# A hybrid attention and RWKV-7 block: the last v projection, the last bonus' split tiles and the first loads of attention and scans change their places

## The chip, the cores and the metric

One core of a Trainium2 chip runs the whole block in one launch. The metric is the device time of one launch in microseconds (us). Lower is better. The profile of an execution also has a span, which is the time from its first to its last recorded instruction. Five engines work side by side: PE multiplies matrices, DVE and ACT work elementwise, POOL (GpSimd) does a few elementwise operations and issues some transfers, and SP issues most transfers. Each engine runs its own instructions strictly in their order; the order is fixed when the kernel is compiled.

## The reference, cut to what matters

```python
h = rms_norm(x, norm_mix)
proj = h @ w_in                      # columns: q, k, v | r, k, v, low ranks | gates
attn = windowed_gqa(q, k, v, sink)   # 8 query heads, 2 key heads, blocks of 128 tokens +-128
zr = zr + shift_mu * (centred_shift(zr) - zr)
rw = rwkv7_time_mix(zr, ...)         # forward and backward scan of 64-wide states, plus
#   bonus = einsum(r, k_dir, r_k) * v
gates = sigmoid(proj[..., O_GATE:])  # 2 x 1024 columns
merged = gates[0] * (attn @ w_up_attn) + gates[1] * (rw @ w_up_rwkv)
x = x + merged @ w_out
x = x + square(relu(rms_norm(x) @ w_ff1)) @ w_ff2
x = x + (p @ w_ple) * sigmoid(rms_norm(x) @ w_ple_gate)
```

There are 1,024 tokens of width 1,024, all in float32. A product is made from three products of split operands (high times high, high times low, low times high), so each weight tile is first split into two parts, `hi` by ACT and `lo` by DVE or POOL.

## The kernel before, in words

The kernel goes through its stages in this order: norm and q, k, v; RWKV preparation; attention; the scans; the merge; the two feed-forward products; the per-layer embedding. The change lies in the end of the preparation and the beginning of the attention, at about 240 to 490 us of the span.

**Preparation.** A loop `for p in range(NP)` treats four pairs of heads (p = 0 to 3). Per pair there are three projections of 48 matmuls each: keys k, receptances r and values v. `shifted` empties their PSUM banks through ACT into the tile `zr` (room for two) and DVE adds the shift. `low_rank` makes the decays and rates, `direction(0, p, ...)` and `direction(1, p, ...)` make each scan direction's operands on DVE and ACT and write them out as `ra_d` and `bk_d`, 1 MB each. `add_bonus` first splits `rk` through `sums2` into high and low halves, multiplies them by ones on PE, transposes v for `v_d`, and writes `bv_d`. The second half's split tiles `s2h` and `s2l` lie in the room `gth` of pool `PW`, which has two places.

**Weights.** `load_proj` loads a projection's weights into pool `PW`, which has two places for split weights and two for the raw halves. `weights_ahead` starts, behind one projection, the load of a later one by the table `ahead2`. For p below 3 that table has k, r and v. For p = 3 it has none of them, so the last v projection loads its weights when it comes up.

**Gate products.** `gates(0)` makes 16 blocks of 24 matmuls each from weights of its own through the same places of `PW`; each block's tanh `gth` lies in the room `gth` until its transfer to `g_d` is done. `fill0` draws matmuls from this generator at fixed places of the last pair, p = 3: before the change 56 ahead of `direction(0, 3)` and the v projection, 56 behind the second `low_rank`, and 12 at each of four loads of `kT`. That makes 160. The rest (and one block of the second half) has the lowest priority and is placed by the compiler between the attention's own work.

**Attention.** Its tiles open in the room of the preparation, after the last bonus' last transfer. It runs over 8 blocks `n`. Its first loads are the queries `qT` (issued by POOL), the mask `band` and the logits `sink` (issued by ACT before the change), and the values `V` (SP). `low_products` loads `la` and `lb` and multiplies them for the scans' first inverse; its loads and those of the scans' first operands (`rac`, `bkc`) are traced at block 3, and nothing binds them to a place in SP's queue. The put of a block's output is the transfer `at_d`.

The program's order is a priority; a compile-time planner makes each engine's fixed order out of it. `after(a, b)` places `a` behind `b` on one engine, and no engine waits for it at run time.

Of the kernel before, what the change touches and what calls it, by code (L numbers as in the profile page):

```python
# [9 lines left out]
F32 = mybir.dt.float32  # L10
F32R = mybir.dt.float32r
# [6 lines left out]
P = 128  # L18
# [6 lines left out]
NP = 4  # L25
NH = 8
# [5 lines left out]
EPS = 1e-6  # L32
LOW = 1000000
X1AT = 5
BQ = 'scalar'
WOAT = (0, 4)

NFS = {2: "s0", 3: "c0 s1", 4: "t0 c1 t1 s2 c2", 5: "t2 s3 c3", 6: "t3 s4 c4", 7: "s5 c5"}
# [11 lines left out]
N1AT = 5  # L50
SQPIN = (1, 2, 3, 4, 5, 6, 7)
TPB = 2
F0 = (56, 56, 12)

FILL0 = 4

# [81 lines left out]
def block_kernel(ctx: ExitStack, tc: tile.TileContext, I: dict, out: bass.AP):  # L138
    nc = tc.nc

    def pool(stack, name, bufs=1, **kw):
        return stack.enter_context(tc.tile_pool(name=name, bufs=bufs, reuse_waits="tile", **kw))
# [9 lines left out]
    ra_d = DR.tile([ND, NCH, P, NP, P], F32, name="ra_d")  # L152
    bk_d = DR.tile([ND, NCH, P, NP, P], F32, name="bk_d")
# [3 lines left out]
    at_d = DR.tile([P, NP, T], F32, name="at_d")  # L157
# [20 lines left out]
    def after(ins, prev):  # L178

        tc.add_manual_dep(  # L180
            ins.ins, prev.ins.name,
            mybir.DependencyInfo(mybir.DependencyClass.NoSync, mybir.DependencyReason.DATA),
            reason="keep_in_program_order")
# [4 lines left out]
    def split(hi, lo, src, lo_eng=None, pin=False):  # L188

        a = nc.scalar.copy(hi, src)  # L190
        b = (lo_eng or nc.vector).tensor_tensor(out=lo, in0=src, in1=hi.bitcast(F32), op=ALU.subtract)  # L191
        if lo_eng is nc.gpsimd:
            on_pool[0] = b
        if pin:
            tc.keep_in_program_order(a)
            tc.keep_in_program_order(b)
# [78 lines left out]
    ahead2, ready = {}, {}  # L275
    for p in range(NP):
        k_, r_, v_ = (O_RWKV + o_ + p * P for o_ in (512, 0, 1024))
        if p < NP - 1:
            ahead2[k_], ahead2[r_], ahead2[v_] = v_, k_ + P, r_ + P

    def load_proj(c):
        ready[c] = load_w(PW, "w", w_in[:, :, c:c + P], P, parts=2, lo_eng=nc.vector)
# [40 lines left out]
    with ExitStack() as s0:  # L323
# [45 lines left out]
        qkn = QW.tile([P, 648], F32, name="qkn")  # L369
# [52 lines left out]
        for t in range(NT):  # L422
# [3 lines left out]
            if t == NT - 1:  # L426
                sA.close()
                PW = pool(sW, "wA", side="right")
# [65 lines left out]
    one_r = G.tile([P, P], F32R, name="one_r")  # L494
# [7 lines left out]
    with ExitStack() as s1:  # L502
        A1 = pool(s1, "prep")
# [82 lines left out]

        s2 = A1.tile([P, 2, 512], F32R, name="s2")

        def sums2(w, src):

            halves = []
            for h in range(2):
                hs = slice(512 * h, 512 * h + 512)
                if h:
                    hi, lo = (PW.tile([P, 512], F32R, name=n, tag="gth", bufs=2) for n in ("s2h", "s2l"))
                else:
                    hi, lo = s2[:, 0], s2[:, 1]
                split(hi, lo, src[:, hs])
                halves.append((hs, hi, lo))
            yield  # L600
            pss = []
            for hs, hi, lo in halves:
                ps = PX.tile([P, 512], F32, name="px", tag="px", bufs=6)
                nc.tensor.matmul(ps, w, hi, start=True, stop=False)
                nc.tensor.matmul(ps, w, lo, start=False, stop=True)
                pss.append((hs, ps))
            yield pss

        def add_bonus(p, rk, vz):
            sums = sums2(one_r, rk)  # L610
            next(sums)
            yield

            vt = A1.tile([P, NT, P], F32, name="vt", bufs=1)
            for q in range(2):
                tp = PX.tile([P, 4, P], F32, name="vtp", tag="px", bufs=6)
                for j in range(4):
                    nc.tensor.transpose(tp[:, j, :], vz[:, (4 * q + j) * P:(4 * q + j + 1) * P], ident)
                nc.scalar.copy(vt[:, 4 * q:4 * q + 4, :], tp)
            nc.sync.dma_start(v_d[:, p * P:(p + 1) * P].rearrange("(t q) c -> q t c", q=P), vt)  # L620
            bv = A1.tile([P, T], F32, name="bv", tag="vt", bufs=1)
            for hs, ps in next(sums):
                nc.vector.tensor_tensor(out=bv[:, hs], in0=ps, in1=vz[:, hs], op=ALU.mult)
            nc.sync.dma_start(bv_d[p], bv)
            yield
# [3 lines left out]
        def fill0(p, i):  # L629

            if p == NP - 1:
                for _ in range(F0[i]):
                    next(gates0)
# [15 lines left out]
        def keys(p):  # L649

            kz = shifted(O_RWKV + 512 + p * P, 4 + p)
            nc.scalar.activation(out=nrm[:, 0], in_=kz, func=AF.Square, scale=col("k_k", p))
            sums = sums2(one_r, nrm[:, 0])
            next(sums)
            return kz, sums
# [65 lines left out]
        for p in range(NP):  # L721
            if bonus:
                next(bonus)

            fill0(p, 0)
            rk = A1.tile([P, T], F32, name="rk", bufs=1)
            direction(0, p, *ops, rk)
            vz = shifted(O_RWKV + 1024 + p * P, 8 + p, proj_with(O_RWKV + 1024 + p * P, {VH: lambda: bonus and next(bonus)}))
            th, ta = low_rank(p, 1)
            fill0(p, 1)  # L730
            nxt = keys(p + 1) if p + 1 < NP else None
            direction(1, p, decays(1, th), ta, *ops[2:], rk)
            bonus = add_bonus(p, rk, vz)
            if nxt:
                ops = normed_keys(p + 1, *nxt)

        kT = PY.tile([P, 2, 2, T], F32R, name="kT", tag="yk")
        for q in range(4):
            ts = slice(256 * q, 256 * q + 256)
            a = nc.gpsimd.dma_start(kT[:, :, :, ts], kT_d[:, :, :, ts])  # L740
            if q:
                after(a, on_pool[0])
            fill0(NP - 1, 2)
        for _ in bonus:
            pass

# [6 lines left out]
    def chunk(s, d):  # L753
        return s if d == 0 else NCH - 1 - s
# [5 lines left out]
        nc.gpsimd.memset(z[64:96, :, 32:64], 0.0)  # L760
        return z

    def low_products(pl, ps_of, b, mm):

        def load(ci):
            la, lb = ([pl.tile([P, NP, 64], F32, name=n, bufs=4) for _ in range(ND)] for n in ("la", "lb"))
            for d in range(ND):
                c = chunk(NB * b + ci, d)
                nc.sync.dma_start(la[d], ra_d[d, c][:, :, 0:64])
                nc.sync.dma_start(lb[d], bk_d[d, c][:, :, 64 * d:64 * d + 64])  # L770
            return la, lb

        nxt = load(0)
        yield
        lt = pl.tile([P, 32, 64], F32, name="lt", bufs=1)
        for ci in range(NB):
            la, lb = nxt
            pss = [ps_of([P, NP, 64], "lps") for _ in range(2)]
            for j in range(NP):
                for q in range(2):  # L780
                    for d in range(ND):
                        e = q ^ d
                        rows = slice(64 * e, 64 * e + 64)
                        l_, r_ = (lb, la) if d == 0 else (la, lb)
                        mm(pss[e][own[d], j, :], l_[d][rows, j, :], r_[d][rows, j, :], start=True, stop=True)
            for e in range(2):
                nc.scalar.copy(lt[:, 8 * ci + e:8 * ci + 8:2, :], pss[e])
            if ci + 1 < NB:
                nxt = load(ci + 1)
            yield lt  # L790
# [60 lines left out]
    BI = pool(sB, "inv")  # L851
    BP = pool(sB, "prod")

    NRA, NBK = 4, 3
    ra_t, bk_t = {}, {}
# [8 lines left out]
    operand_tiles(BP, (0, 1), (0,))  # L864

    def load_ra(s, d):
        nc.sync.dma_start(ra_t[s % NRA, d], ra_d[d, chunk(s, d)])

    def load_bk(s, d):
        nc.sync.dma_start(bk_t[s % NBK, d], bk_d[d, chunk(s, d)])  # L870

    lts, zzs, lows = {}, {}, {}
    with ExitStack() as s2:
        A2 = pool(s2, "att")
# [5 lines left out]
        def queries(n):  # L880
            qT = A2.tile([P, NH, P], F32R, name="qT", bufs=2)
            nc.gpsimd.dma_start(qT, qT_d[n])
            return qT

        qT0 = queries(0)
        low0 = low_products(BI, ps_att, 0, nc.tensor.matmul)
        band = A2.tile([P, 3, P], F32, name="band")
        getattr(nc, BQ).dma_start(band, I["band"])
        V = A2.tile([P, NT, P], F32, name="V")
        nc.sync.dma_start(V, va_d.rearrange("(t q) c -> q t c", q=P))  # L890
        A3 = A2
        sink = A3.tile([P, NH], F32, name="sink")
        getattr(nc, BQ).dma_start(sink, I["qkn"][:, 640:648].partition_broadcast(P))
        nsink = A3.tile([P, NH], F32, name="nsink")
        nc.vector.tensor_scalar_mul(nsink, sink, -1.0)
        for n in range(NT):
# [5 lines left out]
            for kv in range(2):  # L902
# [3 lines left out]
                sums = A3.tile([P, 4], F32, name="sums", bufs=2)  # L906
                es = A3.tile([P, 4], F32, name="es", bufs=2)
                sm = A3.tile([P, 4, 3 * P], F32, name="smk", bufs=2)
                for h in range(4):
                    sc = PA.tile([P, nk * P], F32, name="sc", tag="sc", bufs=2)  # L910
                    for j in range(2):
# [3 lines left out]
                        scalar=-3.0e38, op0=ALU.add, op1=ALU.max, accum_out=mx[:, h:h + 1])  # L915
# [25 lines left out]
                    nc.tensor.matmul(po[kv * 64:kv * 64 + 64], V[:, k0 + j, kv * 64:kv * 64 + 64], pTs[kv][:, j, :, :], start=(j == 0), stop=(j == nk - 1))  # L941
            at = A3.tile([P, 4, P], F32, name="at", bufs=1)
            nc.scalar.copy(at, po)
            nc.sync.dma_start(at_d[:, :, n * P:(n + 1) * P], at)
            if n == 1:
                zi = zi_tile(BI, "zi")
            if n == LOW_AT:
                lts[0] = list(low0)[-1]
                for d in range(ND):
                    load_ra(0, d)  # L950
                    load_bk(0, d)
            if n == INV_AT:
                zzs[0] = inverse_turned(BI, inverse(BI, lts[0]))
        with tc.high_priority(offset=-LOW):
# [293 lines left out]
    for s in range(NCH):  # L1248
# [39 lines left out]
        if s % NB == NB - 1 and s // NB < 3:  # L1288
            b = s // NB + 1
# [615 lines left out]
```

## Time and profile before

| | |
|---|---|
| Median of three runs | 1773.99 us (1770.4 to 1774.12) |
| The profiled execution: its time and its span | 1774.3 us, 1772.5 us |
| PE busy | 1683.0 us, 95% |
| DVE busy | 1139.9 us, 64% |
| ACT busy | 895.5 us, 51% |
| POOL busy | 212.8 us, 12% |
| Mean granted TensorE clock | 0.978 of full speed |

The execution's own time is 1.8 us longer than its span. PE's busy time counts matmuls whose ends are modelled, so 95% doesn't say that PE is at its peak, but it says that PE is seldom empty. The waits of PE are few, and they can be looked up one by one.

### The profile page before, as it was taken

The numbers are of one execution on the slowest core, as the hardware profiler recorded it, in microseconds if no ns is written. First come the engines' busy times: TensorE is split into PE (matmuls) and PEld (weight loads), VectorE is DVE, ScalarE is ACT, GpSimd is POOL, SyncE is SP. The second block draws the span as 40 slices with busy tenths as digits, with TensorE's granted clock in tenths as the row PEclk, the third lists the DMA queues.
The fourth block names the chain that finished last, engine by engine and source line by source line (L and its number), as shares of the span: only waits on it lengthen the run. The fifth ranks groups of instructions, "written<-read, shape, count | busy, mean of one in ns | idle before, by whom it ended". The sixth has DMA issues, their size and how long they took to land. (4 is left out here: it accounts for less than half of the span.)

```text
span 1772.5 us, 29961 instructions
## 1 busy us (share of the span) xinstructions
PE 1683.0 (95%) x11544; PEld 1353.8 (76%) x11544; DVE 1139.9 (64%) x1977; ACT 895.5 (51%) x1636; POOL 212.8 (12%) x210
## 2 busy tenths in 40 slices
PE   7999999799999989898889989999999999999998
PEld 7987776565587777776668867888888888888887
DVE  6658994376928383956662587776776877685432
ACT  5548885277655646474621454444444444554221
POOL 3330000411221221121322000000000000000000
PEclk9999999899999999988989989999999999999999
DMA  6354654855264454355653305444447973574111
GB/s 213 92 133 125 186 159 144 247 148 137 71 181 138 130 142 127 109 162 173 210 187 120 131 32 195 154 148 156 155 144 275 307 246 114 180 225 144 53 42 43
DMA packets 274239, 269.20 MB, mean 152 GB/s; under 512 B 47920, under 2 KB 196272, under 8 KB 274096
## 3 DMA queue, kind: packets, MB, share of 16 engines
q1 hardware_dynamic: 263872, 253.98, 46.1%
q0 software_dynamic: 9792, 12.59, 2.7%
q8 instruction: 91, 1.49, 0.4%
q10 hardware_dynamic: 432, 0.73, 0.1%
q14 instruction: 52, 0.43, 0.1%
HBM read 186.49 MB, written 80.74 MB: 151 GB/s over the span
## 5 line engine op out<-in xcount | busy, mean ns | idle before, releaser
L1787 PE MATMUL ff2ps<-tl,sh 128*128 128x512 f32 x448 | 174.4, 389 | 0.0
L1787 PE MATMUL ff2ps<-th,sl 128*128 128x512 f32 x448 | 174.3, 389 | 0.0
L1787 PE MATMUL ff2ps<-th,sh 128*128 128x512 f32 x448 | 173.9, 389 | 0.0
L191 POOL TENSOR_TENSOR wlo<-wst,whi 128x512 fp32r<-128x512 f32 x66 | 89.1, 1361 | 259.7 <-ACT whi L190 228.1
L190 ACT CAST sh<-sst 128x512 fp32r<-128x512 f32 x109 | 67.8, 622 | 102.4 <-PE ff2ps L1787 56.9
L175 POOL TENSOR_TENSOR rstd<-ms,neghalf 128x1 f32<-128x1 f32 x24 | 13.3, 555 | 792.3 <-DVE ms L173 792.3
L191 DVE TENSOR_TENSOR sl<-sst,sh 128x512 fp32r<-128x512 f32 x109 | 75.1, 689 | 46.9 <-ACT sh L190 46.6
L1787 PEld LDWEIGHTS ff2ps<-tl,sh 128*128 128x128 f32 x448 | 84.1, 188 | 18.0 <-DVE tl L191 0.4
L1787 PEld LDWEIGHTS ff2ps<-th,sh 128*128 128x128 f32 x448 | 84.0, 188 | 17.6 <-ACT th L190 0.3
L1787 PEld LDWEIGHTS ff2ps<-th,sl 128*128 128x128 f32 x448 | 84.1, 188 | 17.5
L190 ACT CAST whi<-wst 128x512 fp32r<-128x512 f32 x100 | 59.7, 617 | 55.6 <-DMA wst<-in_w_in_dram 23.0
L190 ACT CAST w1h<-w1st 128x512 fp32r<-128x512 f32 x48 | 28.4, 620 | 103.8 <-DMA w1st<-in_w_ff_dram 63.9
L191 DVE TENSOR_TENSOR w1l<-w1st,w1h 128x512 fp32r<-128x512 f32 x48 | 31.8, 688 | 50.7 <-ACT w1h L190 50.7
L1112 DVE TENSOR_TENSOR gm<-gps,gmask 128x512 f32<-128x512 f32 x64 | 42.2, 684 | 28.3 <-PE gps L213 28.3
L223 PE MATMUL gmm<-hh,wlo 128*128 128x512 f32 x136 | 56.2, 413 | 1.0 <-DVE wlo L191 0.7
L219 PE MATMUL gmm<-hh,whi 128*128 128x512 f32 x136 | 55.8, 410 | 1.3 <-ACT gth L316 1.3
L221 PE MATMUL gmm<-hl,whi 128*128 128x512 f32 x136 | 56.6, 416 | 0.0
L807 DVE TENSOR_TENSOR tmp<-Lp,Z 128x31 f32<-128x31 f32 (+15 forms) x124 | 52.0, 420 | 4.6 <-POOL Z L802 1.8
L191 DVE TENSOR_TENSOR w1l<-ssum,w1h 128x512 fp32r<-128x512 f32 x64 | 43.0, 687 | 16.1 <-ACT w1h L190 16.1
L1537 PE MATMUL ff1ps<-fh,w1l 128*128 128x512 f32 x128 | 51.0, 399 | 0.6 <-DVE w1l L191 0.6
L1537 PE MATMUL ff1ps<-rh,w1h 128*128 128x512 f32 x128 | 50.0, 391 | 1.7 <-ACT w1h L190 1.7
L213 PE MATMUL gmm<-hh,wlo 128*128 128x512 f32 x120 | 51.3, 428 | 0.0
(410 smaller groups left out, 4937.3 us busy)
## 6 DMA issues: line engine op xcount, KB each, us to landing
wst<-in_w_in_dram SPq DMA_DIRECT2D x92, 256.0 KB, 3.4
tst<-in_w_ff_dram SPq DMA_DIRECT2D x80, 256.0 KB, 4.0
w1st<-in_w_ff_dram SPq DMA_DIRECT2D x32, 512.0 KB, 5.1
hid_S<-h SPq DMA_DIRECT2D x64, 256.0 KB, 2.1
sst<-hid_S SPq DMA_DIRECT2D x64, 256.0 KB, 2.8
hid_A<-h SPq DMA_DIRECT2D x48, 256.0 KB, 2.1
sst<-hid_A SPq DMA_DIRECT2D x45, 256.0 KB, 3.8
ra_d<-ra SPq DMA_DIRECT2D x8, 1024.0 KB, 5.7
```

What stands on the lines that cost most here:

```text
L175: nc.gpsimd.tensor_tensor(out=r, in0=ms, in1=neghalf.broadcast_to([P, width]), op=ALU.pow)
L190: a = nc.scalar.copy(hi, src)
L191: b = (lo_eng or nc.vector).tensor_tensor(out=lo, in0=src, in1=hi.bitcast(F32), op=ALU.subtract)
L213: tc.keep_in_program_order(nc.tensor.matmul(*a, **kw))
L219: mm(ps, ah, bh, start=(i == 0), stop=False)
L221: mm(ps, ah, bl, start=False, stop=False)
L223: mm(ps, al, bh, start=False, stop=(i == n - 1))
L807: nc.vector.tensor_tensor(out=tv, in0=Lp[:, t + 1:32, t:t + 1].broadcast_to([P, n, m]), in1=Z[:, t:t + 1, 0:m].broadcast_to([P, n, m]), op ...
L1112: nc.vector.tensor_tensor(out=gm[d][:, s % NB, q::2, :], in0=pss[q], in1=gmask[:, d, :].unsqueeze(1).broadcast_to([P, NP, P]), op=ALU.mult)
L1537: nc.tensor.matmul(ps, x_[:, k, :], y_[:, k, :], start=start and k + i == 0, stop=k == 3 and i == 2, skip_group_check=True)
L1787: nc.tensor.matmul(banks[bs][i], x_[:, isl], y_, start=fresh and p + j == 0, stop=p == NPR - 1 and j == 2, skip_group_check=True)
```

## The change

Four edits belong to it. The last v projection's weights are loaded behind the last k projection (`ahead2` gets `k_` for p = 3 too). The first 56 of the gate products move from ahead of `direction(0, 3)` to behind the second `low_rank`, so that 112 stand there. The last bonus' `s2h` and `s2l` go from the room `gth` to the room `zr` of pool `A1`. `band` and `sink` are issued by SP ahead of everything else of the attention, the scans' `la` and `lb` loads stand behind the put of block 0, and the first `rac` and `bkc` loads behind that of block 3.

```diff
-F0 = (56, 56, 12)
+F0 = (112, 12)
...
     for p in range(NP):
         k_, r_, v_ = (O_RWKV + o_ + p * P for o_ in (512, 0, 1024))
+        ahead2[k_] = v_
         if p < NP - 1:
-            ahead2[k_], ahead2[r_], ahead2[v_] = v_, k_ + P, r_ + P
+            ahead2[r_], ahead2[v_] = k_ + P, r_ + P
...
-        def sums2(w, src):
+        def sums2(w, src, pool_tag=(PW, "gth")):
...
-                    hi, lo = (PW.tile([P, 512], F32R, name=n, tag="gth", bufs=2) for n in ("s2h", "s2l"))
+                    hi, lo = (pool_tag[0].tile([P, 512], F32R, name=n, tag=pool_tag[1], bufs=2) for n in ("s2h", "s2l"))
...
-            sums = sums2(one_r, rk)
+            sums = sums2(one_r, rk, (A1, "zr") if p == NP - 1 else (PW, "gth"))
...
-            fill0(p, 0)
             rk = A1.tile([P, T], F32, name="rk", bufs=1)
             direction(0, p, *ops, rk)
             vz = shifted(O_RWKV + 1024 + p * P, 8 + p, proj_with(O_RWKV + 1024 + p * P, {VH: lambda: bonus and next(bonus)}))
             th, ta = low_rank(p, 1)
-            fill0(p, 1)
+            fill0(p, 0)
...
-            fill0(NP - 1, 2)
+            fill0(NP - 1, 1)
...
-    def low_products(pl, ps_of, b, mm):
+    def low_products(pl, ps_of, b, mm, behind=None):
...
-                nc.sync.dma_start(la[d], ra_d[d, c][:, :, 0:64])
-                nc.sync.dma_start(lb[d], bk_d[d, c][:, :, 64 * d:64 * d + 64])
+                for a in (nc.sync.dma_start(la[d], ra_d[d, c][:, :, 0:64]),
+                          nc.sync.dma_start(lb[d], bk_d[d, c][:, :, 64 * d:64 * d + 64])):
+                    if behind:
+                        after(a, behind)
...
+        band = A2.tile([P, 3, P], F32, name="band")
+        nc.sync.dma_start(band, I["band"])
+        sink = A2.tile([P, NH], F32, name="sink")
+        nc.sync.dma_start(sink, I["qkn"][:, 640:648].partition_broadcast(P))
         qT0 = queries(0)
-        low0 = low_products(BI, ps_att, 0, nc.tensor.matmul)
-        band = A2.tile([P, 3, P], F32, name="band")
-        getattr(nc, BQ).dma_start(band, I["band"])
         V = A2.tile([P, NT, P], F32, name="V")
         nc.sync.dma_start(V, va_d.rearrange("(t q) c -> q t c", q=P))
...
-            nc.sync.dma_start(at_d[:, :, n * P:(n + 1) * P], at)
+            put = nc.sync.dma_start(at_d[:, :, n * P:(n + 1) * P], at)
+            if n == 0:
+                low0 = low_products(BI, ps_att, 0, nc.tensor.matmul, put)
+                next(low0)
...
                 for d in range(ND):
-                    load_ra(0, d)
-                    load_bk(0, d)
+                    for a in (load_ra(0, d), load_bk(0, d)):
+                        after(a, put)
```

## Rows read from the trace of the kernel before

**Rows 1.** The page's chain that ended last: shares of the span by engine.

```profile
PE 46%; DVE 1%; ACT 0%; DMA 0%; issue 0%; POOL 0%; DVEq 0%; ACTq 0%; POOLq 0%
```

**Rows 2.** Waits of PE, 250 to 500 us: total us, times, longest us.

```profile
PE px L604 <- ACT s2h L190: 8.3, 1, 8.3
...
PE mm L219 <- ACT whi L190: 2.3, 1, 2.3
PE gmm L219 <- ACT gth L316: 1.3, 1, 1.3
...
PE gmm L223 <- DVE wlo L191: 0.7, 1, 0.7
```

**Rows 3.** Windows: stretch, length, busy PE PEld DVE ACT POOL, PEclk, DMA, GB/s.

```profile
250.00:260.00 10.00, 10.00 (x45) 7.61 (x44) 10.00 (x9) 8.21 (x12) 0.00 (x0) 1.00 0.69 209
...
326.00:341.20 15.20, 6.87 (x19) 4.77 (x18) 1.98 (x3) 3.70 (x7) 2.50 (x2) 0.67 0.90 262
...
350.60:493.00 142.40, 130.60 (x718) 85.28 (x716) 101.62 (x322) 97.24 (x256) 30.62 (x32) 0.96 0.46 131
```

**Rows 4.** Timeline of ACT and of its own transfer queue (ACTq).

```profile
334.30 0.62 ACT L190 CAST s2h<-rk 128x512 fp32r<-128x512 f32 x1 [9.70 <-DMA g_d<-gth]
...
346.33 0.33 ACTq L888 DMA_DIRECT2D band<-in_band_dram  x1
```

**Rows 5.** Timeline of DVE.

```profile
322.22 1.23 DVE L715 TENSOR_TENSOR rk<-rk,z 128x1024 f32<-128x1024 f32 x1
...
339.35 1.29 DVE L623 TENSOR_TENSOR bv<-px,z 128x512 f32<-128x512 f32 x2 [3.57 <-DMA v_d<-vt]
...
353.11 0.17 DVE L895 TENSOR_SCALAR nsink<-sink 128x8 f32<-128x8 f32 x1 [12.47 <-DMA sink<-in_qkn_dram]
```

**Rows 6.** Windows of the gate matmuls alone: length, PE busy, PEclk, DMA, GB/s.

```profile
303.00:326.00 23.00, 21.38 (x89) 1.00 0.72 188
...
336.40:350.50 14.10, 14.07 (x51) 0.83 0.81 261
```

**Rows 7.** Timeline of PE: start us, us, what, [idle before <- releaser].

```profile
265.63 0.40 PE L219 MATMUL gmm<-hh,whi 128*128 128x512 f32 x1
...
290.30 0.80 PE L219 MATMUL mm<-hh,whi 128*128 128x512 f32 x1 [2.30 <-ACT whi L190]
...
293.45 0.42 PE L219 MATMUL mm<-hh,whi 128*128 128x512 f32 x1
...
301.98 1.09 PE L213 MATMUL px<-lr,wlrh 128*128 128x512 f32 x4
...
325.21 1.04 PE L618 MATMUL vtp<-ident,z 128*128 128x128 f32 x8
...
334.97 0.79 PE L604 MATMUL px<-s2h,one_r 128*128 128x512 f32 x1 [8.25 <-ACT s2h L190]
...
341.13 0.48 PE L219 MATMUL gmm<-hh,whi 128*128 128x512 f32 x1
...
350.56 0.63 PE L912 MATMUL sc<-kT,qT 128*128 128x256 f32 x4
...
353.78 0.51 PE L912 MATMUL sc<-kT,qT 128*128 128x256 f32 x2 [2.12 <-DVE mx L913]
```

**Rows 8.** Timeline of SP's transfer queue.

```profile
335.92 0.37 SPq L620 DMA_DIRECT2D v_d<-vt  x1
...
341.14 0.38 SPq L624 DMA_DIRECT2D bv_d<-bv  x1
```

**Rows 9.** Timeline of POOL.

```profile
344.24 1.12 POOL L882 DMA_DIRECT2D qT<-qT_d  x2
```

**Rows 10.** DMA issues, 326 to 352 us: count, KB each, median us to landing.

```profile
band<-in_band_dram ACTq DMA_DIRECT2D x1, 192.0 KB, 6.0
```

**Rows 11.** Instructions that read tile la: ns min/median/max, first to last start us.

```profile
L785 PE MATMUL lps<-la,lb x34: 218/218/267, 408.0 to 416.7; 64*64 64x64 f32 x34
```

**Rows 12.** Instructions of line 944, the puts of the attention's blocks.

```profile
L944 SPq DMA_DIRECT2D at_d<-at x8: 525/558/622, 369.0 to 485.5; - x8
```

More of the change, by code (lines that the diff above doesn't have):

```diff
@@ L34 @@
 X1AT = 5
-BQ = 'scalar'
 WOAT = (0, 4)
@@ L866, in load_ra @@
     def load_ra(s, d):
-        nc.sync.dma_start(ra_t[s % NRA, d], ra_d[d, chunk(s, d)])
+        return nc.sync.dma_start(ra_t[s % NRA, d], ra_d[d, chunk(s, d)])
     def load_bk(s, d):
-        nc.sync.dma_start(bk_t[s % NBK, d], bk_d[d, chunk(s, d)])
+        return nc.sync.dma_start(bk_t[s % NBK, d], bk_d[d, chunk(s, d)])
     lts, zzs, lows = {}, {}, {}
@@ L891, in block_kernel @@
         A3 = A2
-        sink = A3.tile([P, NH], F32, name="sink")
-        getattr(nc, BQ).dma_start(sink, I["qkn"][:, 640:648].partition_broadcast(P))
         nsink = A3.tile([P, NH], F32, name="nsink")
```

## The prediction

> **What bounds the kernel now.** The first view is the page's chain of work. Its shares add up to 47% and nearly all of it is PE [rows 1]. 47% of the span of 1772.5 us is some 833 us, so the chain ends, followed back, at about 940 us. It says that the second half of the kernel waits for PE alone. It says nothing of the preparation's end, which lies at 265 to 350 us. So the second view is the list of PE's waits there [rows 2]. Two of them are large, and both belong to things that the change touches: 8.3 us at the last bonus' second product, which waits for the high part `s2h`, and 2.3 us at the last v projection, which waits for its weights. The third view, the windows, shows what that does: from 326 to 341.2 us PE works for 6.87 of 15.2 us, at 0.67 of its clock, while DVE (1.98 us) and ACT (3.70 us) are nearly empty too [rows 3]. All engines stand still for one thing. The fourth view is ACT's timeline, which names it: the cast of `s2h` waits 9.70 us for the transfer `g_d<-gth`, since `s2h` needs a place in the room `gth` that a gate's tanh leaves only when it has been written out [rows 4]. `rk`, from which `s2h` is made, was ready at 322.22 + 1.23 = 323.45 us [rows 5]. It is the room that is late and not the data.
>
> **Is time won here won at the end?** From 350.6 to 493 us PE is busy for 130.6 of 142.4 us, DVE for 101.62 and ACT for 97.24 [rows 3]. PE's remaining 11.8 us are spread over many small waits. Whatever starts the attention earlier moves this stretch as a whole, because the same work follows: the number of gate matmuls drawn before it is 160 before and after the change (56 + 56 + 48, and 112 + 48). The scans and everything behind them follow in their fixed order. So I let a gain here pass to the end in full.
>
> **The change part by part.**
>
> *Price of a matmul and of the clock.* 89 gate matmuls took 21.38 us at full clock, 0.240 us each [rows 6]. Behind the 2.30 us gap PE starts 7 matmuls from 290.30 to 293.45 us, so 0.450 us each, 0.210 more: 7 x 0.210 = 1.47 us. That is the price of the 1.2 GHz level against 2.4 GHz there. Behind the 8.25 us gap 13 starts lie between 334.97 and 341.13 us [rows 7], 6.16 us where 13 x 0.240 = 3.12 would do, so 3.04 us.
>
> *The last v projection.* With `ahead2` for p = 3 its weights follow the k projection's, in the places that the first gate block's weights have now, and those were in time. So the 2.30 us and the 1.47 us behind them go: 3.77 us. The 56 moved matmuls cost the same at either place. The wait of 1.3 us for a tanh [rows 2] belongs to the same crowding: that tanh stands on ACT behind the previous bonus' copies, which will now fall into the v projection. I count 1.31 us as gone; the bounds are 0 and 1.31.
>
> *What moves forward with it.* The second `low_rank` now stands at 301.98 us, and `rk` is ready 21.5 us later, at 323.45 [rows 5, 7]. After the change it follows the v projection directly: r's product ends and the gates begin at 265.63 [rows 7], v takes 48 x 0.240 = 11.5, the bonus inside it 1.04 + 4 x 0.240 = 2.0, so `low_rank` begins at about 279 and `rk` is ready at about 301. The bonus itself keeps its place behind 160 gate matmuls. These begin behind `low_rank` (1.09 us for its first half, some 1.8 in all), and 160 x 0.240 = 38.4 us later it is 319. The bonus now begins at 325.21 [rows 7]. `rk` has some 18 us to spare.
>
> *The cost of that.* The lo parts of the first five gate blocks are made on DVE, and four of them now meet `direction(1, 3)` there. The nearest row is the wait for such a part, 0.7 us [rows 2]. Four such waits would cost 2.7 us, none 0; the splits are traced first and so have priority, and I take 1.0.
>
> *The bonus' room.* The room `zr` is free when the bonus comes: its two places were last used by the r and v projections, whose shift is over by about 282 us (279 and two operations of 1.23 us on DVE). So the 8.25 us and the 3.04 us behind them go: 11.29 us. The gates get both places of `gth` back, which I count at nothing, because no other wait for that room is in the list.
>
> *The attention's start.* It opens when `bv_d` has landed. From the issue of `v_d` at 335.92 over `bv` at 339.35, `bv_d` at 341.14 and `qT` at 344.24 to the first score at 350.56 it takes 14.64 us [rows 5, 7, 8, 9]. PE has 51 gate matmuls to cover it [rows 6], 12.2 us at full clock. Now they run partly at the lower clock and last 14.07. So a wait of up to 14.64 - 12.2 = 2.4 us can show in front of the first score, and with it up to 1.47 us of clock. With less of a queue of transfers (DMA share 0.90 now [rows 3]) all four landings may come earlier, and then it is 0. I take 1.5 of 0 to 3.9 us.
>
> *`band` and `sink`.* ACT issues them at 346.33 us, 2.09 us after POOL issues the queries at 344.24 [rows 4, 9], because a tanh stands ahead of them on ACT. DVE waits for them until 353.11 [rows 5], and PE's third score waits 2.12 us for DVE [rows 7]. Issued first by SP they go out with the queries, so I count 2.09 us and, as behind the 2.30 us gap, 1.47 us of clock. The bounds are 0 and 3.6.
> The transfer of `band` took 6.0 us on ACT's own queue [rows 10]. The Trainium skill, "DMA: Bandwidth & Descriptors", section "Queues, rings and completion order", says that every DMA engine takes turns between the queues, while within one queue descriptors are consumed in ring order. That speaks against the move: behind two weight loads of 256 KB in SP's queue `band` would, by an estimate from that page's rule and 262 GB/s [rows 3], land 2.0 us later, and the sum would be smaller by the 3.6 us of this item: 1760.5 instead of 1757. No row shows `band` on SP's queue.
>
> *The scans' loads.* `la` and `lb` are read from 408.0 us [rows 11]; behind the first put, at 369.0 [rows 12], they have 39 us. `rac` and `bkc` come behind block 3's put and are used by the scans, behind the last put at 485.5 [rows 12]. The cover is the attention itself. Without it a load would cost a landing like that of `band`, 6.0 us. On SP the weights of the next gate blocks move up, which I count at nothing.
>
> *Sum.* -3.77 - 1.31 + 1.0 - 11.29 + 1.5 - 2.09 - 1.47 = -17.4 us. From the profiled execution's 1774.3 us that makes 1756.9; I say 1757. The median of the runs, 1773.99, differs from that execution by 0.3 us.
>
> **The rivals.**
>
> *A. The wait changes its name.* PE's gap stays in part: the first score or the gate blocks' weights wait where `s2h` did. For it: after the bonus SP's queue holds loads that need the attention's room, and weights behind them wait as well. `bv_d` goes out 5.2 us behind `v_d`, and the room opens 3.1 us later [rows 8, 9]: 8.3 us. Against it: the weights in front of `V` now pass in time. Of the 17.4 us some 9 remain, 1765.
>
> *B. No change that can be measured.* The attention could be bound by something that doesn't move with it, and PE's gap would reappear among its 11.8 us [rows 3]. DVE is busy for 71% of that stretch, so it would have to be one place of it. Time: 1771 to 1777. Differences within 0.2%, 3.5 us, can't be told from none.
>
> *C. Slower: DVE becomes the bound at the turn to the last pair.* At 250 to 260 us DVE is busy for all of 10 us and ACT for 8.21 [rows 3]. The change brings the shift of v, the scan, nine operations of the second direction and four gate splits there at once: by an estimate from the length of L715, 1.23 us [rows 5], thirteen such and eight of half the length, 21 us of DVE work in the 22 us from 279 to 301. If the planner puts the splits behind the direction's operations, each of the four blocks waits for its weights. It decides from 17.4 / 4 = 4.4 us a block on, three and a half such operations. With 6 us a block it would be 4 x 6 - 17.4 = 6.6 us slower, 1781. Against it: the one wait for such a part is 0.7 us long.
>
> *D. More.* If the attention's small waits shrink with the emptier queue, or the first score needn't wait, 5 to 10 us more go: 1747 to 1752.
>
> **How the numbers follow.** The forecast, 1752 to 1764 us, gets 0.60: its lower end has the two new waits at nothing (1757 - 1.0 - 1.5 = 1754.5) and some of the 11.8 us gone as well, its upper end has three of them against me (1.3 for the tanh, 3.6 for `band` and 1.7 for DVE, 1763.6). A gets 0.15, B 0.08, C 0.12, D 0.05. The range is 1750 to 1770: it holds the forecast, A and part of D. Faster by over 0.2% are the forecast, A and D, 0.80; the same is B, 0.08; slower is C, 0.12.
>
> **What the profile after would show.** Right: no wait of `px` for `s2h` and none of `mm` for `whi` in PE's list; v's matmuls directly behind r's, without gates between; the bonus' first transpose at about 319 us and the first score at about 334; the windows around both at a clock of 1.00. The `band` item is right if the first mask operation on DVE comes within a microsecond of the first score. Wrong would be: a gap of PE of several microseconds in front of the first score (A), gate matmuls that wait for `wlo` again and again at 280 to 305 us (C), or a first score that is 15 us earlier while the scans' first product isn't (B). The prediction would fail in its main term if the planner gave the bonus another place, so that the room `zr` or `rk` were late there.

## The result and the profile after

| | before | after |
|---|---|---|
| median of the runs compared | 1774.12 us | 1762.06 us |
| ratio, 95% interval | | 0.9929 [0.9911, 0.9947] |
| profiled execution: time, span | 1774.3, 1772.5 us | 1762.2, 1760.4 us |
| mean granted clock | 0.978 | 0.980 |

The change makes the kernel faster by 0.7%: 0.0071 x 1774.12 = 12.6 us. Run a second time in another session (after_again, below) it gave 0.9918 [0.9901, 0.9935], 14.5 us. The forecast was 17.4 us.

PE's list of waits from 250 to 500 us in the kernel after (total us, times, longest us) answers to [rows 2]:

```profile
PE sc L912 <- DMA qT<-qT_d: 6.9, 1, 6.9
PE pt L933 <- DVE smk L930: 2.6, 7, 0.7
PE gmm L218 <- ACT whi L189: 2.5, 1, 2.5
```

The wait for `s2h` (8.3 us), that of `mm` for `whi` (2.3) and that for the tanh (1.3) are gone. Two others stand there: 6.9 us in front of the first score and 2.5 us inside the gates. The prediction had named a gap of several microseconds in front of the first score as the sign of its rival A, so by that sign a part of A came true.

Windows of the kernel after (stretch, length, busy PE, PEld, DVE, ACT, POOL, PEclk, DMA share, GB/s), the first for a stretch of [rows 3], the second from the first score to the scans' first product:

```profile
326.00:341.20 15.20, 14.10 (x65) 11.18 (x62) 1.29 (x2) 5.69 (x10) 7.37 (x7) 1.00 0.81 235
...
346.99:479.62 132.63, 127.52 (x715) 83.78 (x715) 97.36 (x322) 96.44 (x256) 27.88 (x27) 0.99 0.47 129
```

Where PE stood still for half of the time before, from 326 to 341.2 us, it is now busy for 14.10 of 15.2 us. The attention's stretch, 350.56 to 493.01 us before, is 142.45 us long there and 132.63 us here, with 715 matmul rows in it against 719. PE's idle time in it falls from 11.8 to 5.1 us; the rest is its busy time, 130.65 and 127.52 us, at a granted clock of 0.96 and 0.99. The profile of after_again has the clock of 0.96, 137.35 us of stretch and 6.6 us idle.

PE's timeline of the kernel after, with the places of [rows 7]:

```profile
294.91 0.50 PE L218 MATMUL gmm<-hh,whi 128*128 128x512 f32 x1 [2.53 <-ACT whi L189]
...
298.78 0.41 PE L218 MATMUL gmm<-hh,whi 128*128 128x512 f32 x1
...
325.74 1.03 PE L618 MATMUL vtp<-ident,z 128*128 128x128 f32 x8
...
327.30 0.39 PE L605 MATMUL px<-s2l,one_r 128*128 128x512 f32 x1
...
346.99 1.19 PE L912 MATMUL sc<-kT,qT 128*128 128x256 f32 x4 [6.89 <-DMA qT<-qT_d]
...
350.07 0.39 PE L218 MATMUL gmm<-hh,whi 128*128 128x512 f32 x1
```

All times of this execution are 3.5 us late from the start on (the last section), so the bonus' first transpose is at 322.2 on the scale of before and the first score at 343.5; after_again has them at 322.3 and 342.3. Forecast were 319 and 334. What stands between bonus and score is read from the other engines. ACT, SP's queue, DVE and POOL of the kernel after:

```profile
294.24 0.62 ACT L189 CAST whi<-wst 128x512 fp32r<-128x512 f32 x1 [4.03 <-DMA wst<-in_w_in_dram]
...
329.58 0.62 ACT L189 CAST whi<-wst 128x512 fp32r<-128x512 f32 x1 [2.36 <-DMA wst<-in_w_in_dram]
330.10 1.07 ACT L619 COPY vt<-vtp 128x512 f32<-128x512 f32 x2
```

```profile
328.61 3.35 SPq L206 DMA_DIRECT2D wst<-in_w_in_dram  x2
332.01 0.50 SPq L620 DMA_DIRECT2D v_d<-vt  x1
...
338.03 0.34 SPq L624 DMA_DIRECT2D bv_d<-bv  x1
...
339.83 0.45 SPq L887 DMA_DIRECT2D band<-in_band_dram  x1
```

```profile
305.34 1.22 DVE L715 TENSOR_TENSOR rk<-rk,z 128x1024 f32<-128x1024 f32 x1
...
347.19 0.17 DVE L895 TENSOR_SCALAR nsink<-sink 128x8 f32<-128x8 f32 x1 [9.19 <-DMA sink<-in_qkn_dram]
347.79 0.43 DVE L913 CUSTOM_DVE_ANT_0 smk<-sc,band 128x256 f32<-128x256 f32 x1 [0.43 <-PE sc L912]
```

```profile
338.99 1.28 POOL L190 TENSOR_TENSOR wlo<-wst,whi 128x512 fp32r<-128x512 f32 x1 [2.16 <-ACT whi L189]
340.22 1.12 POOL L883 DMA_DIRECT2D qT<-qT_d  x2
```

From the issue of `v_d` (332.01) to the first score (346.99) it takes 14.98 us; the prediction had 14.64. But `v_d` goes out 4.5 us behind the bonus' last product, which begins at 327.30 and after which the gates go on at 327.53: the copies of `vt` stand on ACT behind a cast that waits 2.36 us for weights, and `v_d` stands in SP's queue behind two weight loads. Further on, `band` goes out 1.8 us behind `bv_d`, and the queries 2.2 us behind `bv_d`, as POOL's lo part in front of them waited 2.16 us for `whi`. So the way is 346.99 - 327.53 = 19.46 us, and 53 gate matmuls of 0.237 us cover 12.6 of it.

In the kernel before, the same two queues looked like this (ACT, then SP):

```profile
334.82 1.07 ACT L619 COPY vt<-vtp 128x512 f32<-128x512 f32 x2
```

```profile
328.27 1.94 SPq L207 DMA_DIRECT2D wst<-in_w_in_dram  x2
```

The two weight loads ahead of `v_d` went out inside the stall of 8.25 us. On ACT `vt` was copied right behind the cast of `s2h` [rows 4], and the weights' casts came behind it. That a weight's cast now stands ahead of `vt` is a new order of the planner.

### The profile page after: what moved, and what is told of

The parts are those of the page before. It is cut to its first block, busy times and chain, and to the rows that moved or that the text cites. A ratio compares the mean times of both kernels' runs of the same rounds, so it can differ in the third digit from the quotient of the medians.

```text
span 1760.4 us, 29968 instructions
## 1 busy us (share of the span) xinstructions
PE 1679.0 (95%) x11544; PEld 1352.9 (77%) x11544; DVE 1129.6 (64%) x1977; ACT 895.6 (51%) x1636; POOL 209.7 (12%) x210
```

## The experiments

Times are against the kernel before, run in the same session (1773 to 1774 us).

### The parts alone, and two together

e1_room has only the other room, e2_vproj only the v projection's weights and the gates behind it, e3_loads only the edits of the loads, e4_room_vproj the first two. Their edits are those of the diff of the change; in short:

```
e1   sums = sums2(one_r, rk, (A1, "zr") if p == NP - 1 else (PW, "gth"))
e2   ahead2[k_] = v_          # for all p
e2   F0 = (112, 12)           # one block of gates behind the v projection
e3   band, sink by nc.sync ahead of queries(0); la, lb, rac, bkc after(a, put)
```

> The kernel before with one edit: the last bonus' s2h and s2l lie in the room zr. Sum theory (the prediction's terms add up): the 8.25 us wait and the 3.04 us of clock go, about 3 us come back in front of the first score: 8 us faster, 1766. Chain theory (the attention opens a fixed way behind the bonus, and that way sets the end): the bonus starts at the same 325 us, and with 14.6 to 19 us behind it the first score comes at 341 to 346 us instead of 350.6: 5 to 9 us faster, with a new wait of PE for qT of several us. Queue theory (the room was late only because the transfer of the tanh stood behind the 2 MB of ra_d and bk_d): same as the sum theory here.

> The kernel before with one edit: the last v projection's weights ahead, its product ahead of the gate products. Sum theory: 2.30 + 1.47 + 1.31 - 1.0 us, 4 us faster, 1770, and the wait for s2h stays near 8 us. Queue theory: ra_d and bk_d of the last direction are now written some 20 us before the bonus, the tanh's transfer lands at once, and the wait for s2h shrinks to 3 us or less by itself: 9 to 12 us faster, 1763. Chain theory: between the two, as the bonus starts no earlier than 3 us before.

> The kernel before with one edit: band and sink first on SP, the scans' loads behind the puts. Sum theory: 2.09 + 1.47 us, 3.6 us faster, 1770.5. If the landing on SP's queue is later by as much as the issue is earlier: no change. If the scans' loads were what held back qT and the gates' weights: more than 4 us faster, and qT lands in 4 us instead of 6.

> The whole change without the loads' edit: band and sink on ACT's queue, the scans' loads where they were. Sum theory: 3.6 us slower than the whole change, 1765. Chain theory: the first score waits for qT in any case, and band lands in that wait, so it is as fast as the whole change, 1762. If the scans' loads cost qT its bandwidth: 1766 and a longer wait for qT than 6.9 us.

| | ratio, 95% interval | us |
|---|---|---|
| e1_room | 0.9984 [0.9973, 0.9996] | -2.8 |
| e2_vproj | 0.9957 [0.9944, 0.9969] | -7.6 |
| e3_loads | 0.9967 [0.9954, 0.9979] | -5.9 |
| e4_room_vproj | 0.9927 [0.9914, 0.9940] | -12.9 |

The shares of the parts are not those of the prediction's sum. The room alone, forecast at 11.3 us, gives 2.8. What happened to it is in PE's list of waits, ACT's timeline and SP's queue of e1_room:

```profile
PE gmm L219 <- ACT whi L190: 7.7, 1, 7.7
```

```profile
325.18 0.61 ACT L190 CAST s2h<-rk 128x512 fp32r<-128x512 f32 x1
...
336.04 1.38 ACT L190 CAST whi<-wst 128x512 fp32r<-128x512 f32 x2 [8.78 <-DMA wst<-in_w_in_dram]
```

```profile
318.34 0.50 SPq L716 DMA_DIRECT2D ra_d<-ra  x1
320.14 2.75 SPq L717 DMA_DIRECT2D bk_d<-bk  x1
322.98 6.39 SPq L317 DMA_DIRECT2D g_d<-gth  x2
329.47 2.52 SPq L207 DMA_DIRECT2D wst<-in_w_in_dram  x2
```

`s2h` is cast at 325.18, without a wait for its place: the room does what it was to do. But in SP's queue stand the last direction's two writes of 1 MB each and two writes of gates, and the next weights go out at 329.47 only. The second gate's tanh was done at 326.29, 3.1 us before its write had been issued. The weights' cast then starts 6.57 us behind their issue, where weights in this stretch land in 3.6 us (median). PE waits 7.7 us for them instead of 8.3 for `s2h`. The edit of the v projection acts on that queue: it brings the last direction forward. In e2_vproj these writes go out at 298.09 and 303.71, and the wait for the split tiles shrinks without any change of their room:

```profile
PE sc L912 <- DMA qT<-qT_d: 4.3, 1, 4.3
PE px L606 <- DVE s2l L191: 3.1, 1, 3.1
```

So the queue theory holds for the gap at 326 us: the traffic of the last direction was late, and the room decided only under which name PE waited for it. How much of it is the late issue and how much the slow landing isn't taken apart. e3_loads gives 5.9 us alone and nothing that can be told on top of the other two (0.9927 without it, 0.9929 and 0.9918 with it).

### One part left out

```
e5   without (A1, "zr"): the split tiles stay in (PW, "gth")
e6   without ahead2[k_] = v_; F0 = (56, 56, 12)
```

> The whole change once more, beside the kernels that leave one part of it out. Every theory: -12 us against the kernel before, 1762 us, and in front of the attention's first score a wait of 6 to 7 us for the queries.

> The whole change without the room zr: the last bonus' split tiles stay in the gates' room. The prediction's sum gives the room 11.3 us, less what the earlier v projection already took of its wait (e2_vproj left 3.1 us of it): at least 3 us slower than the whole change, 1765. The queue theory: what is late is the traffic in the transfer queue, which the room only moves to another wait; without the room PE waits some 3 us for s2h and as much less for the queries, so the same as the whole change within 1.5 us, 1762.

> The whole change with the v projection back behind its 56 gate products. The prediction's sum gives the v projection 3.8 us: 1766. The queue theory: the last direction's writes are back at 318 to 323 us, so the gates' weights or the queries are waited for, as in e1_room (7.7 us); the parts alone add up to -2.8 - 5.9 = -8.7 us, 1765, and if both parts lean on the same idle time it is less, 1768 (e3_loads alone).

| | ratio, 95% interval | us |
|---|---|---|
| after_again | 0.9918 [0.9901, 0.9935] | -14.5 |
| e5_vproj_loads | 0.9943 [0.9928, 0.9959] | -10.1 |
| e6_room_loads | 0.9972 [0.9955, 0.9988] | -5.0 |

On top of the other two parts the v projection is worth 14.5 - 5.0 = 9.5 us and the room 14.5 - 10.1 = 4.4 us, though the intervals of after_again and e5_vproj_loads overlap. The queue theory had expected nothing from the room here, as the waits would trade places. They do so only in part:

```profile
PE px L606 <- DVE s2l L191: 3.9, 1, 3.9
PE sc L913 <- DMA qT<-qT_d: 3.2, 1, 3.2
```

These are 7.1 us in e5_vproj_loads against 5.6 us for the queries alone in after_again. The bonus' first transpose comes at 322.89 and 322.75 us in the two profiles, the first score at 347.05 and 342.72: 4.2 us of the difference lie between the two, which is about what the room gives. e6_room_loads shows the gap of e1_room again:

```profile
PE gmm L219 <- ACT whi L190: 7.3, 1, 7.3
```

### More work beside the bonus' way

e7_cover is the whole change with the last bonus ahead of the keys' loop, and with 80 instead of 53 gate matmuls behind it.

```
F0 = (112, 20)
...
            if q == 0:
                for _ in bonus:
                    pass
            fill0(NP - 1, 1)
```

> The whole change, with the last bonus ahead of the keys' loop and 80 gate products instead of 53 between it and the first score. Cover theory: the 6.9 us in front of the first score are the way of 19.3 us from the last bonus over vt, v_d, bv and bv_d to the queries, less the 53 x 0.24 = 12.4 us of products that stand beside it; 80 x 0.24 = 19.2 us cover it all, the wait falls below 1 us, and with it some of the clock: -5 to -8 us against the whole change, 1754 to 1757. Queue theory: the queries are late for the traffic, whatever stands beside them; the first score comes at the same 347 us, the wait only moves to a gate's weights, 1761 to 1763.

It gave 0.9954 [0.9937, 0.9970], 8.2 us faster than before and slower than the whole change beside it (after_again). The longest of PE's waits, and a row each of its timeline and of ACT's:

```profile
PE gmm L218 <- ACT whi L189: 7.9, 2, 5.4
```

```profile
332.49 0.71 PE L913 MATMUL sc<-kT,qT 128*128 128x256 f32 x4 [1.58 <-DMA qT<-qT_d]
```

```profile
337.95 0.62 ACT L189 CAST whi<-wst 128x512 fp32r<-128x512 f32 x1 [11.35 <-DMA wst<-in_w_in_dram]
```

Both theories are half right. The wait for the queries falls from 5.6 (after_again) to 1.6 us, so most of that wait was the uncovered rest of the bonus' way. The first score comes 10 us earlier; some 5 us of this is work put off, as 192 gate matmuls stand ahead of it where there were 213. But the next gate's weights, issued behind `V` and two loads of the scans in SP's queue, are then 5.4 us late.

### The two halves of the loads

e3a_band is the kernel before with `band` and `sink` issued first by SP; e3b_scan is the kernel before with only the scans' loads put behind the blocks.

```
e3a  nc.sync.dma_start(band, I["band"])      # band and sink ahead of queries(0)
e3b  low0 = low_products(BI, ps_att, 0, nc.tensor.matmul, put)   # behind block 0's put
```

> The kernel before with band and sink alone issued first by SP; the scans' loads stay. The prediction's sum: -3.6 us (2.1 us of wait and 1.5 us of clock), 1769 to 1770; by the ring-order rule band lands later than it did on ACT's queue and nothing is won, 1773. The loads' edit as a whole (e3_loads) gave -5.9 us: if band is what counts in it, -4 to -6 us here.

> The kernel before with the scans' first loads alone put behind the attention's blocks. The prediction counts them at nothing: 1773. Queue theory: 1.5 MB of loads less beside the queries and the gates' weights at 340 to 350 us, so -1 to -4 us, 1769 to 1772, and a gain at the gates' weights or smk rather than in front of the first score.

They gave 0.9988 [0.9976, 1.0000], 2.1 us, and 0.9986 [0.9970, 1.0003], 2.5 us. Neither is told from no change for certain; together, in e3_loads, they are. The wait that the `band` item was to remove is still in e3a_band's list, 2.1 us longest before and 2.5 here:

```profile
PE sc L912 <- DVE mx L913: 2.8, 2, 2.5
```

Its cause is DVE's first operation of the attention, here in e3a_band and, for comparison, in e4_room_vproj, which has `band` and `sink` still on ACT's queue:

```profile
352.85 0.17 DVE L895 TENSOR_SCALAR nsink<-sink 128x8 f32<-128x8 f32 x1 [12.07 <-DMA sink<-in_qkn_dram]
```

```profile
342.62 0.17 DVE L895 TENSOR_SCALAR nsink<-sink 128x8 f32<-128x8 f32 x1 [8.98 <-DMA sink<-in_qkn_dram]
```

In e3a_band SP issues `sink` at 345.61, 1.1 us earlier than ACT did, and it is there at 352.85, 0.26 us earlier than before [rows 5]. In e4_room_vproj ACT issues `band` at 335.94, 0.35 us ahead of the queries, since no tanh stands in the way there; `sink` is there at 342.62 and the first score waits until 343.98. The stall that this edit is about is already gone when the other two are made.

The scans' half changes something else, at the attention's far end. PE's waits for `smk` before and in e3b_scan:

```profile
PE pt L933 <- DVE smk L930: 5.9, 5, 3.1
```

```profile
PE pt L934 <- DVE smk L931: 2.4, 5, 0.7
```

In e3a_band, e1_room and e2_vproj it is 5.8 us as before, the longest 3.1. That longest wait is one operation of DVE which lasts 3.15 us, beside two splits and two memsets of POOL (before):

```profile
475.57 3.15 DVE L930 TENSOR_SCALAR smk<-smk,es 128x256 f32<-128x256 f32 x1
```

```profile
474.22 2.58 POOL L191 TENSOR_TENSOR wlo<-wst,whi 128x512 fp32r<-128x512 f32 x2 [7.20 <-ACT whi L190]
476.74 1.84 POOL L1097 MEMSET Sb<- 128x1024 f32 x2
```

In e3b_scan the same operation takes 0.34 us, at 474.50, and none of POOL's stands beside it: its split at 472.98 is over at 474.42. So the edit wins something by another order on DVE and POOL, and not by a load that lands earlier. It is an order that another edit can undo: e9_clear_cover (below) has this half too and waits 5.6 us for `smk`.

### Less traffic beside the queries, and both together

e8_clear is the whole change with `V` behind the first queries in POOL's queue, and the scans' second chunk behind the fourth block's put. e9_clear_cover has e7_cover's order as well.

```
after(nc.gpsimd.dma_start(V, va_d.rearrange("(t q) c -> q t c", q=P)), on_q[0])
...
            r = load_ra(s, d)
            if s == 1:
                after(r, put_low)
```

> The whole change, with V behind the first queries in POOL's queue instead of SP's, and with the two loads of the scans' second chunk behind the fourth block's put. 1 MB less is then under way beside the queries. Queue theory: the first queries land 2 to 3 us sooner, the wait in front of the first score falls from 5.6 to 6.9 us to some 4 us, -2 to -4 us against the whole change, ratio 0.990. Chain theory: the queries are late because the bonus' way is long, so the wait keeps its length within 1 us and the time that of the whole change, 0.9918 to 0.9929.

> The last kernel with the last bonus ahead of the keys' loop as in e7_cover, 80 gate products between it and the first score. In e7_cover the wait for the queries went (1.6 us left) but the next gate's weights were 5.4 us late behind V and the scans' loads. Queue theory: with these out of the way the weights come in time as well, no wait of over 3 us between 285 and 360 us, ratio 0.988 to 0.990. If PE's order itself (fewer gate products in front of the attention, more inside it) is what cost e7_cover its gain: 0.994 to 0.996 again.

e8_clear gave 0.9926 [0.9909, 0.9943], the time of the whole change. The queries are not a bit sooner, as PE's waits and the list of DMA issues (330 to 352 us) show:

```profile
PE sc L915 <- DMA qT<-qT_d: 5.9, 1, 5.9
```

```profile
qT<-qT_d POOLq DMA_DIRECT2D x2, 512.0 KB, 7.8
```

The 7.8 us are the median of the first two loads, 7.3 in the kernel after; the first alone lands 6.6 us behind its issue in both. What the queue theory forecast didn't come, and the chain theory's forecast did. But the edit clears less than its expectation says: POOL issues `V` at 339.99, 0.58 us behind the first queries, so `V` still moves beside them, and only the scans' two loads, 0.5 MB, are out of the way. e9_clear_cover gave 0.9910 [0.9895, 0.9925], 16.0 us faster than before, and its waits up to the first score are short (that for `smk` lies in the attention):

```profile
PE pt L937 <- DVE smk L934: 5.6, 5, 2.9
PE gmm L218 <- ACT whi L189: 2.6, 1, 2.6
...
PE sc L916 <- DMA qT<-qT_d: 0.9, 1, 0.9
```

Against e7_cover it differs only in `V` and the two loads, and the intervals are apart: that traffic cost e7_cover its gain. It did so by late weights above all (7.9 us of waits against 2.6), and by the queries a little (1.6 against 0.9): `V` goes out 3.1 us behind them here and 0.04 us in e7_cover, and they land in 5.6 us here and in 7.0 there. The forecast was 0.988 to 0.990. Against the whole change (0.9918 and 0.9929) it has the lowest median, 1757.21 us, but the intervals overlap, so that it beats it is not shown.

## Why the prediction was right, and where its numbers were not

The direction and the range were right; the time is 5 us (1.7 us in the second session) above the forecast. That it is no more is luck in part: two terms came out 10 us worse than counted, and part of this was made up for by a gain that the sum doesn't have (below). Rival A came by its own sign, the gap in front of the first score, but not at its price: it left 9 of the 17.4 us, and the measured 12.6 and 14.5 us lie between it and the forecast. Step by step:

- *The last v projection.* v's matmuls follow r's directly, and the wait of 2.30 us is gone, with the tanh's. Right in mechanism, too small in value: the 3.8 us count only what PE waits there. Bringing the last direction forward also takes its writes out of the queue before the bonus; alone the edit gave 7.6 us.
- *The bonus' room.* The wait for `s2h` went as forecast, and `zr` was free. The 11.3 us were wrong as the room's own: the step "it is the room that is late and not the data" stopped at the first cause. Behind the late room stood a late queue, and alone the room gave 2.8 us. That is rival A: in e1_room PE waits for the gates' weights instead. In the whole change the v projection clears the queue, and there the room is worth 4.4 us, with intervals that overlap.
- *The attention's start.* This is the term that failed by most: 1.5 us, with 3.9 as the upper bound. Measured are 6.89 us of wait and some clock: from 346.99 to 350.07 lie eight score matmuls of 256 columns, worth four gate matmuls, and three gate matmuls, 7 x 0.240 = 1.68 us of work in 3.08 us, so 1.4 us more. Together 8.3 us. The chain from `v_d` on was right (14.98 us against 14.64). But it was counted from `v_d`'s issue, as if that went out with the bonus' last product. Before the change it did: `vt` was copied at 334.82, as the stall ended, and `v_d` went out at 335.92 with the last product at 335.84. The weight loads ahead of `v_d` in SP's queue had gone out (328.27) during the very stall of 8.25 us that the change removes. Without it they show, and on ACT a weight's cast now stands ahead of `vt`, which before came behind it: together 4.5 us. e7_cover and e9_clear_cover bear out that the way is too long for its cover, since more gate matmuls at this place take the wait down to 1.6 and 0.9 us.
- *DVE's lo parts.* Forecast 1.0 us. No wait for `wlo` came. Instead a gate block waited 2.53 us for `whi`, whose weights landed late (ACT's row at 294.24): they went out at 286.74, behind the `bv_d` of the pair before, and took 7.3 us to land (median of two). Behind the wait nine matmuls took 3.87 us where 9 x 0.240 = 2.16 would do, so it is 4.2 us in all. Rival C, DVE as the bound, did not come about: `rk` was ready at 306.56, or 303.1 on the scale of before, against 301 forecast.
- *`band` and `sink`.* By the prediction's own sign the item is right: the first mask operation comes at 347.79, 0.8 us behind the first score. But the sign would have come without the edit: in e4_room_vproj, where the tanh that held ACT's issue is out of the way, `sink` is there before the first score. Alone the edit left the wait where it was (2.5 us) and gave 2.1 us, with an interval that reaches to no change. So the 3.6 us of this item are not its own. The Trainium skill, "DMA: Bandwidth & Descriptors", section "Queues, rings and completion order", says that descriptors of one queue are consumed in ring order. For `sink` e3a_band agrees as far as it goes: issued 1.1 us earlier, behind SP's other loads, it arrived 0.26 us earlier. For `band` the prediction's estimate of a landing 2.0 us later isn't borne out: it landed in 5.4 us in e3a_band and in 3.1 in the kernel after, against 6.0 on ACT's queue. In the kernel after, `sink` came 0.2 us behind the first score's start and held nothing up, so that there the rule cost nothing.
- *The scans' loads.* The one wait of PE for them, that of `lps` for `lb`, is 1.9 us before and 1.7 after (3.1 in after_again), so the cover of 39 us holds but for that. Moving them off gave 2.5 us (0 within its interval) where nothing was counted. It took 3.5 us from PE's waits for `smk` (e3b_scan).
- *What made up for it.* The two new waits cost 8.3 + 4.2 = 12.5 us where 2.5 were counted, 10.0 more, so -7.4 us would be left of -17.4. Measured are -12.6 and -14.5. The rest is in the attention's stretch: 142.45 us before, 132.63 after, 137.35 in after_again, so 5.1 to 9.8 us less, of which `band`'s 3.6 were counted; that adds 1.5 to 6.2 us, and -8.9 to -13.6 us come out. Rival D named this as smaller waits in the attention. Idle time of PE is 5.2 to 6.7 us of it, and the wait for `smk`, 5.9 us before and 2.6 after, is the largest piece. The scans' half alone brings it to 2.4 us, but the two other edits alone also bring it to 3.0 (e4_room_vproj). In the kernel after, 3.1 us more are busy time at a higher granted clock, which after_again doesn't show. Which edit shortened which of the small waits in the whole change stays open.
- *The way to the end.* The scans' first product comes at 479.62 instead of 493.01 us, 13.4 us earlier, and the profiled execution is 12.1 us shorter. That a gain here passes to the end holds within 1.3 us.

## What to carry to other kernels

Before a stall is removed, look at what else lies inside it on every engine: the issues and transfers that it covers come out with it, the planner may order the rest anew, and both belong in the sum, from the last instruction ahead of the stall and not from where the next chain happens to start. A wait for a buffer behind a full transfer queue changes its name when it gets another buffer; the lever is what keeps the queue full. Measure the parts of such a change alone and left out, for a right total can have wrong shares: the room, counted at 11.3 us, gave 2.8 alone, and the v projection with what belongs to it, counted at some 4 us, gave 7.6.

## What the runs showed of the hardware

The landing of the same load differs with what runs beside it. From its issue to its landing the first load of the queries, 512 KB, took 5.0 us (e1_room) to 7.6 us (e4_room_vproj). The nearest pair is e7_cover and e9_clear_cover, which differ only in `V` and the scans' two loads:

```profile
qT<-qT_d POOLq DMA_DIRECT2D x1, 512.0 KB, 7.0
```

```profile
qT<-qT_d POOLq DMA_DIRECT2D x1, 512.0 KB, 5.6
```

That is 1.4 us, by one execution of each. The Trainium skill, "DMA: Bandwidth & Descriptors", section "Anatomy of one DMA — SWDGE (gpsimd) path", has 2.0 us plus the bytes at 436 GB/s for a transfer that GpSimd issues, by an estimate from it 3.2 us for 512 KB. No landing of this load near the first score was so short.

DVE's operations on 128x1024 last longer beside POOL's. Two of DVE's rows before and one of POOL's there, then the second of DVE's lines after, where POOL makes no lo parts:

```profile
318.74 1.21 DVE L710 TENSOR_TENSOR bk<-kd,Ei 128x1024 f32<-128x1024 f32 x1
319.88 2.31 DVE L714 SCALAR_TENSOR_TENSOR rk<-kd,pc,rk 128x1024 f32<-128x1024 f32 x1
```

```profile
319.23 1.87 POOL L191 TENSOR_TENSOR wlo<-wst,whi 128x512 fp32r<-128x512 f32 x1
```

```profile
303.06 1.27 DVE L714 SCALAR_TENSOR_TENSOR rk<-kd,pc,rk 128x1024 f32<-128x1024 f32 x1
```

It is 2.31 against 1.27 us on DVE, and 1.87 against 1.28 us on POOL, whose split begins while DVE's first operation is still running. The Trainium skill, "SBUF — State Buffer", section "Terms", says that both arbitrate for a shared pair of ports and that the loser blocks; the rows agree, in that POOL's split, begun inside DVE's L710, and DVE's L714, begun inside the split, each last longer, while L710, which was there first, doesn't. After the change the last direction meets gate blocks whose lo parts DVE makes itself, at 0.69 us each, and three of its long operations (L703, L709, L714) are 1.0 to 1.1 us shorter each.

The same instructions can start late. PE's order is the same in both kernels up to the bonus ahead of the last pair (265 us before, 269 after). Yet the first `low_rank` begins at 133.6 us before and at 137.1 after (134.0 in after_again). From 10 to 30 us and from 105 to 115 us the granted clock is 0.91 and 0.83 after, and 1.00 in both before and in after_again. Inside the second stretch PE waits once, for 1.62 us before, 1.83 after and 1.97 in after_again, so the length of that wait alone doesn't tell the two apart. The delay comes and goes between executions of one kernel, so times of two profiles are compared from a common point on.
